# Forgetting attention with the decay tiles in ten buffers, loaded and masked four groups ahead

## Chip, cores and metric

The kernel runs on one core of one Trainium2 chip. The metric is device time in microseconds (us) of one launch. TensorE (PE) multiplies matrices and loads their stationary operand (PEld), VectorE (DVE) and ScalarE (ACT) do the elementwise work, GpSimd (POOL) here issues DMAs and a few additions, SyncE (SP) issues the weight loads.

## What is computed

A two-layer decoder trunk on 256 tokens of width 1024, in float32. Every layer is half a feed-forward block, a token mixer, and another half feed-forward block. The mixer of the second layer, which the change touches, is attention with a learned decay:

```python
decay = transpose(Fqb)[..., None] - F_k[:, :, None, :]      # F: running sums of log forget gates
logits = einsum('bqhd,bkhd->bhqk', qb, k) * scale + decay
logits = where(causal, logits, -inf)
p = softmax(logits, axis=-1)
o = einsum('bhqk,bkhd->bqhd', p, v)                         # then x = x + gate * (o @ w_o)
```

There are 16 heads of width 64, and the queries come in two blocks of 128. The first query block sees 128 keys, the second sees 256, so a head has 384 columns of logits.

## The kernel before

Every large weight matrix streams from HBM in pieces of up to 1024 columns. SP loads a piece into one of six `raw` buffers. ScalarE casts it into a high half `wh` (six buffers), VectorE forms the low half `wl = raw - wh` (five buffers), and each product is three TensorE instructions: high by high, low by high, high by low. TensorE is therefore busy nearly all the time, and the two other engines work as its feeders.

A planner, class `InOrder`, writes out the instructions of TensorE, ScalarE, VectorE and SP in a fixed order. It keeps an estimated clock for each engine and puts casts and `wl` subtractions where it expects an engine to be idle. DMAs issued with `nc.gpsimd` go past it: the compiler's own scheduler places them in POOL's queue, and the planner does not see how long they take.

`attention_b` is the stage of the change. Heads go in pairs; pair `c` is one of eight. First `late_pairs` computes the first half of the queries. Then groups 0 to 9 run. Group `t` is three steps of three pairs at once: the scores of pair `t`, the transposes of the softmax weights of pair `t-1`, and the products with the values of pair `t-2`. Before each group TensorE does `n` steps of fill, `n` being 3, 9, 8, 8, 8, 8, 7, 7, 6, 4 in turn. One step is three matmuls. The first 32 steps compute the rest of the queries (tiles `lq`), and from step 33 on they are the output projection (tiles `pw`, class `OutProj`, which needs the outputs `o[k]`). Four more steps follow group 9, and the last eight are mixed into `OutProj.finish`, which adds the result to `x`.

Within a group the orders are these.

- TensorE: `scores` (tiles `sb`), `values` (into the right half of the bank `wb`), `weights_t`, the six transposes (into `wa` and the left half of `wb`).
- VectorE: four logits passes `d = -0.125 * sb + d` with a row minimum (in `exps`), the low half of the outputs `obl` (in `out_split`), the copy `wtb` (in `weights_out`). Two fill steps before the next group `scale` follows, one reciprocal and four multiplications that finish the softmax in `d`.
- ScalarE: four exponentials (in `exps`), the high half of the outputs `obh` (in `out_split`), the copy `wta` (in `weights_out`).

The decay of head `hd` comes into a tile `d` of 384 columns. Line 1236 loads it from HBM with one POOL DMA (192 KB); line 1241 adds the causal mask to two of its three blocks with a second POOL DMA that accumulates (128 KB, `d<-tri` in the profile). The logits pass then overwrites `d`, the exponentials and `scale` too, and the transposes are its last readers. Six buffers serve the 16 heads, three pairs' worth. They are the hidden tiles of the feed-forward block just before (`hidh4` to `hidh7`, `hidl8`, `hidl9`). `decay(0)` and `decay(1)` stand ahead of group 0 in the code, and group `t` ends with `decay(t + 2)`. Output tiles take `hidh0` to `hidh3` and `hidl4` to `hidl7`.

Of the kernel before, what the change touches and what calls it, by code (L numbers as in the profile page):

```python
# [10 lines left out]
F32 = mybir.dt.float32  # L11
F32R = mybir.dt.float32r
BF16 = mybir.dt.bfloat16
AF = mybir.ActivationFunctionType
ALU = mybir.AluOpType
PSUM = bass.MemoryType.PSUM

P = 128
D = 1024
S = 256  # L20
NC = D // P
# [82 lines left out]
def trunk(ctx, tc, a, out):  # L104
# [4 lines left out]
    dve = InOrder(tc, nc.vector, 0.08, 1 / 960)  # L109
    sp = InOrder(tc, nc.sync, 0.0, 1 / 704)  # L110
    cp_ = ctx.enter_context(tc.tile_pool(name="cp", bufs=1))
# [9 lines left out]
    def sbank(name):  # L121
        return pp.tile([P, 512], F32, tag="s", name=name, bufs=2)

    def abank(name):
        return pp.tile([P, 512], F32, tag="ta", name=name)

    def bbank(name):
        return pp.tile([P, 512], F32, tag="tb", name=name)
# [375 lines left out]
    def late_pair(src, dst, r, name):  # L504

        banks = [mmbank(f"{name}{b}") for b in range(2)]
        blk = take(src)
        for k in range(NC):
            for b in range(2):
                mm3(banks[b][:, :SX], blk(k * 256 + b * P), hx[k], k == 0, k == NC - 1)  # L510
            if k == NC - 1:
                late_out(dst, banks, r)
            yield k, NC

    def late_pairs(src, dsts, m, then):

        pb = []
        for i in range(2):  # L520
            banks = [mmbank(f"lp{i}{b}") for b in range(2)]
            pb.append(banks)
            blk = take(src)
            for k in range(NC):
                for b in range(2):
                    mm3(banks[b][:, :SX], blk(k * 256 + b * P), hx[k], k == 0, k == NC - 1)
                if i == 0:
                    if k == 3:
                        r = rstd_of(then)
                        mh = MakeH(r, m) if m else None  # L530
                else:
                    if k == 0:
                        late_out(dsts[0], pb[0], r)
                    if mh:
                        mh.go()
        if mh:
            mh.go(9 - mh.k)
        late_out(dsts[1], pb[1], r)
        mode[0] = "run"
        return r  # L540
# [366 lines left out]
    for k in range(0, NC, 2):  # L907
# [3 lines left out]
        if k % 4:  # L911
            i = k // 4
# [237 lines left out]
    op, rest = attention_a()  # L1150
# [69 lines left out]
    ffn(1, 0, "ready", None, ((1, 4), (1, 3)))  # L1220

    def attention_b():
        ohs = [cp_.tile([P, 512], F32R, tag=f"hidh{j}", name=f"obh{j}") for j in range(4)]
        ols = [cp_.tile([P, 512], F32R, tag=f"hidl{4 + j}", name=f"obl{j}") for j in range(4)]
        o = [(ohs[c // 2][:, (c % 2) * 256:(c % 2) * 256 + 256],
              ols[c // 2][:, (c % 2) * 256:(c % 2) * 256 + 256]) for c in range(NC)]
        q = [cp_.tile([P, 512], F32, tag=f"hidl{j}", name=f"q{j}") for j in range(4)]
        ds, sms = {}, {}

        DT = [f"hidh{4 + j}" for j in range(4)] + ["hidl8", "hidl9"]  # L1230

        def decay(c):

            for hd in (2 * c, 2 * c + 1):
                d = cp_.tile([P, 384], F32, tag=DT[hd % 6], name=f"d{hd}")
                nc.gpsimd.dma_start(d, bass.AP(fdram.tensor, fdram.offset + hd * (P + S), [[0, P], [1, P + S]]))
                ds[hd] = d
            m2 = mask.rearrange("p (o k) -> p o k", o=1).to_broadcast([P, 2, P])
            for hd in (2 * c, 2 * c + 1):
                diag = ds[hd].rearrange("p (b k) -> p b k", k=P)[:, ::2]  # L1240
                nc.gpsimd.dma_start(diag, m2, accum_op=ALU.add)

        r = late_pairs("wq", q[:2], None, AF.Exp)
        for c in range(2):
            decay(c)
        op = OutProj(o)
        st = {}
        mode[0] = "fill"
        NP = BH // 2

        def scores(c, sb):

            cb = (c % 2) * 256
            for qt, (c0, w) in enumerate(QT):
                for m in range(2):
                    rows = slice(m * HD, m * HD + HD)
                    mm(sb[m][:, c0:c0 + w], q[c // 2][rows, cb + qt * P:cb + qt * P + P],
                       kT[c // 2][rows, cb:cb + w], start=True, stop=True)

        def exps(c, sb):  # L1260
            nm = kp.tile([P, 4], F32, tag="nm", name=f"nmb{c}")
            sm = kp.tile([P, 4], F32, tag="smb", name=f"smb{c}", bufs=3)
            for m in range(2):
                d = ds[2 * c + m]
                for qt, (c0, w) in enumerate(QT):
                    cc = 2 * qt + m
                    dve.tensor_tensor_reduce(
                        d[:, c0:c0 + w], sb[m][:, c0:c0 + w], d[:, c0:c0 + w], -0.125, BIG,
                        ALU.add, ALU.min, accum_out=nm[:, cc:cc + 1])
                    act.activation(d[:, c0:c0 + w], d[:, c0:c0 + w], AF.Exp,  # L1270
                                   bias=nm[:, cc:cc + 1], scale=-1.0, accum_out=sm[:, cc:cc + 1])
            sms[c] = sm

        def scale(c):

            rs = kp.tile([P, 4], F32, tag="rs", name=f"rsb{c}")
            dve.reciprocal(rs, sms[c])
            for m in range(2):
                d = ds[2 * c + m]
                for qt, (c0, w) in enumerate(QT):  # L1280
                    dve.tensor_scalar(d[:, c0:c0 + w], d[:, c0:c0 + w], rs[:, 2 * qt + m:2 * qt + m + 1], None,
                                      op0=ALU.mult)

        def weights_t(c, ta, tb):
            for m, b, to, i in ((0, 0, ta, 0), (0, 1, ta, 1), (0, 2, ta, 2), (1, 2, ta, 3), (1, 0, tb, 0), (1, 1, tb, 1)):
                pe.transpose(to[:, i * P:i * P + P], ds[2 * c + m][:, b * P:b * P + P], ident)

        def weights_out(c, ta, tb):
            w0 = cp_.tile([P, 512], F32, tag="hidh8", name=f"wta{c}")
            w1 = cp_.tile([P, 256], F32, tag="hidh9", name=f"wtb{c}")  # L1290
            act.copy(w0, ta)
            dve.tensor_copy(w1, tb[:, :256])
            st[c] = ((w0[:, :2 * P], w0[:, 2 * P:3 * P]), (w1, w0[:, 3 * P:]))

        def values(c, po):

            for kt in range(2):
                for m in range(2):
                    hd = 2 * c + m
                    v = vb[kt][hd // 8][:, (hd % 8) * HD:(hd % 8) * HD + HD]  # L1300
                    mm(po[m * HD:m * HD + HD, kt * P:], v, st[c][m][kt], start=kt == 0, stop=kt == 1)

        def out_split(c, po):
            oh, ol = o[c]
            act.copy(oh, po)
            dve.tensor_tensor(ol, po, oh.bitcast(F32), op=ALU.subtract)

        def group(t):

            cs, cw, cv = (c if 0 <= c < NP else None for c in (t, t - 1, t - 2))  # L1310
            sb = [sbank(f"sb{t}_{m}") for m in range(2)] if cs is not None else None
            ta = abank(f"wa{t}") if cw is not None else None
            tb = bbank(f"wb{t}") if cw is not None or cv is not None else None
            if cs is not None:
                scores(cs, sb)
            if cv is not None:
                values(cv, tb[:, 256:])
            if cw is not None:
                weights_t(cw, ta, tb)
            if cs is not None:  # L1320
                exps(cs, sb)
            if cv is not None:
                out_split(cv, tb[:, 256:])
            if cw is not None:
                weights_out(cw, ta, tb)
            if t + 2 < NP:
                decay(t + 2)

        def fills():
            for j in (2, 3):  # L1330
                for _ in late_pair("wq", q[j], r, f"lq{j}"):
                    yield
                    yield
            for _ in range(6):
                for _ in op.steps():
                    yield

        fill = fills()
        for t, n in enumerate((3, 9, 8, 8, 8, 8, 7, 7, 6, 4)):
            for i in range(n):  # L1340
                if 1 <= t <= NP and i == n - 2:
                    scale(t - 1)
                next(fill)
            group(t)
        for _ in range(4):
            next(fill)
        return op, fill

    pace[0] = PACE[5]
    op, rest = attention_b()  # L1350
    op.finish((1, 5), ((1, 7), (1, 6)), rest)
    pace[0] = PACE[6]
# [130 lines left out]
```

## Time and profile before

| what | value |
|---|---|
| median of 3 runs | 983.62 us (983.29 to 989.06) |
| the profiled execution's own time | 983.71 us |
| its span in the trace | 981.7 us |
| TensorE busy | 962.2 us, 98% |
| VectorE, ScalarE, POOL busy | 820.0, 552.2, 74.5 us |
| HBM read | 264.75 MB |

The span is the part of the execution that the trace covers; 2.0 us lie around it. "Busy" for TensorE counts overlapping matmuls with modelled ends, so its share says little by itself: the spacing of starts, and the stretches without a start, tell more. In the rows below, a bracket after an instruction gives the idle time of its engine just before it and what ended that time. Windows are given in microseconds from the start of the span.

### The profile page before, as it was taken

Reading aid. Unit: us, or ns where it says so; the run is one execution under the profiler, and the core shown is the slowest. Engines: PE = TensorE matmul, PEld = TensorE weight load, DVE = VectorE, ACT = ScalarE, POOL = GpSimd, SP = SyncE. Lnnn points to the kernel's source line nnn. Section 1 sums busy time; section 2 is a strip of 40 time slices with the busy share of each in tenths; the row PEclk is TensorE's granted clock in tenths of the full one; section 3 lists DMA queues with packets and bytes.
Section 4 is the critical chain, followed back from the end, with each engine's and each line's share of the span. In section 5 each row is a group of like instructions: output and inputs, shape, how many; then the busy total and the mean of one; then the engine's idle time right before and its main releaser. Section 6 shows DMA issues by size and latency. Waiting matters only on the chain.

```text
span 981.7 us, 20425 instructions
## 1 busy us (share of the span) xinstructions
PE 962.2 (98%) x8076; PEld 933.6 (95%) x8076; DVE 820.0 (84%) x1372; ACT 552.2 (56%) x894; POOL 74.5 (8%) x110
## 2 busy tenths in 40 slices
PE   8999999999999999999999999999998799999997
PEld 6999999988999999999998999999997699999997
DVE  7989979889999998878898989889976599555575
ACT  4465545576777654555577545545566476445432
POOL 0000100000112000000000000000044213300000
PEclk9999999999999999999999999999999999999999
DMA  9988999958776699789968999979896437978651
GB/s 361 414 344 279 341 375 343 344 208 289 283 237 229 226 379 371 281 279 319 327 209 318 349 334 326 362 276 338 291 294 155 117 126 214 271 142 278 189 153 43
DMA packets 73825, 270.32 MB, mean 275 GB/s; under 512 B 9673, under 2 KB 14577, under 8 KB 63618
## 3 DMA queue, kind: packets, MB, share of 16 engines
q1 hardware_dynamic: 66016, 259.69, 75.2%
q0 software_dynamic: 7424, 9.02, 4.1%
q8 instruction: 63, 1.03, 0.4%
q10 hardware_dynamic: 290, 0.32, 0.1%
q14 instruction: 32, 0.26, 0.1%
HBM read 264.75 MB, written 2.66 MB: 272 GB/s over the span
## 4 chain that ended last, share of the span: by engine, by line
PE 91%; DVE 3%; issue 3%; DMA 1%; POOL 1%; ACT 1%; DVEq 0%; POOLq 0%; ACTq 0%
PE po L99 25%; PE pg L99 21%; PE pu L99 21%; PE pf L99 5%; PE pv L99 5%; PE lp L99 4%; PE pqk L99 3%; PE pw L99 2%; PE pk L99 1%; DVE wl L99 1%; DMA d<-tri 1%; PE lq L99 1%; DVE HL L99 1%; PE s L99 1%; PE lu L99 1%
## 5 line engine op out<-in xcount | busy, mean ns | idle before, releaser
L99 ACT CAST wh<-raw 128x1024 fp32r<-128x1024 f32 (+1 forms) x360 | 347.3, 975 | 209.9 <-PE pu L99 88.3
L99 DVE TENSOR_TENSOR wl<-raw,wh 128x1024 fp32r<-128x1024 f32 (+1 forms) x360 | 398.5, 1125 | 71.9 <-ACT sg L99 20.7
L99 DVE CUSTOM_DVE_ANT_0 ada<-ada,cact,vecs 128x1024 f32<-128x1024 f32 x160 | 203.4, 1278 | 0.3 <-DMA ada<-in_ada 0.3
L99 PE MATMUL pg<-HH,wl 128*128 128x256 f32 x608 | 168.1, 276 | 0.3 <-DVE wl L99 0.3
L99 PE MATMUL pg<-HH,wh 128*128 128x256 f32 x608 | 168.0, 276 | 0.0
L99 PE MATMUL pu<-HH,wh 128*128 128x256 f32 x608 | 167.9, 276 | 0.0
L99 PE MATMUL pu<-HL,wh 128*128 128x256 f32 x608 | 167.9, 276 | 0.0
L99 PE MATMUL pg<-HL,wh 128*128 128x256 f32 x608 | 167.9, 276 | 0.0
L99 PE MATMUL pu<-HH,wl 128*128 128x256 f32 x608 | 167.9, 276 | 0.0
L99 PE MATMUL po<-hidh,wh 128*128 128x256 f32 x528 | 145.7, 276 | 0.0
L99 PE MATMUL po<-hidh,wl 128*128 128x256 f32 x528 | 145.7, 276 | 0.0
L99 PE MATMUL po<-hidl,wh 128*128 128x256 f32 x528 | 145.7, 276 | 0.0
L99 PEld LDWEIGHTS pg<-HH,wh 128*128 128x128 f32 x608 | 114.1, 188 | 0.7 <-issue 0.6
L99 PEld LDWEIGHTS pg<-HH,wl 128*128 128x128 f32 x608 | 114.2, 188 | 0.5 <-DVE wl L99 0.4
L99 PEld LDWEIGHTS pu<-HH,wh 128*128 128x128 f32 x608 | 114.2, 188 | 0.0
L99 PEld LDWEIGHTS pg<-HL,wh 128*128 128x128 f32 x608 | 114.2, 188 | 0.0
L99 PEld LDWEIGHTS pu<-HL,wh 128*128 128x128 f32 x608 | 114.1, 188 | 0.0
L99 PEld LDWEIGHTS pu<-HH,wl 128*128 128x128 f32 x608 | 114.1, 188 | 0.0
L99 PEld LDWEIGHTS po<-hidh,wh 128*128 128x128 f32 x528 | 99.1, 188 | 0.0
L99 PEld LDWEIGHTS po<-hidh,wl 128*128 128x128 f32 x528 | 99.1, 188 | 0.0
L99 PEld LDWEIGHTS po<-hidl,wh 128*128 128x128 f32 x528 | 99.1, 188 | 0.0
L99 ACT CAST hidh<-hf 128x512 fp32r<-128x512 f32 x44 | 27.3, 621 | 40.8 <-DVE hf L99 40.6
(224 smaller groups left out, 1864.7 us busy)
## 6 DMA issues: line engine op xcount, KB each, us to landing
raw<-in_win SPq DMA_DIRECT2D x176, 512.0 KB, 6.7
ada<-in_ada SPq DMA_DIRECT2D x79, 1024.0 KB, 6.9
raw<-in_wout SPq DMA_DIRECT2D x48, 384.0 KB, 5.6
raw<-in_wout SPq DMA_DIRECT2D x48, 320.0 KB, 5.1
raw<-in_wqk SPq DMA_DIRECT2D x16, 512.0 KB, 5.3
raw<-in_wo SPq DMA_DIRECT2D x16, 512.0 KB, 5.8
raw<-in_wlast SPq DMA_DIRECT2D x16, 512.0 KB, 4.1
raw<-in_wv SPq DMA_DIRECT2D x8, 512.0 KB, 7.3
```

Source lines behind the costliest of these rows:

```text
L99: return self.tc.keep_in_program_order(f(*args, **kw))
```

## The change

- The decay tiles get ten buffers in place of six. The four new ones are `hidh2`, `hidh3`, `hidl6` and `hidl7`, which the last two output tiles take later; output tiles are now allocated when they are first written (`o_tiles`).
- Load and mask are separate functions. Ahead of group 0 the loads of pairs 0 to 4 and their masks are issued, loads one pair ahead of masks. Groups 1, 2 and 3 end with load and mask of pairs 5, 6 and 7.
- The copy `obh` on ScalarE moves ahead of the exponentials of the group, and the subtraction `obl` on VectorE moves behind the copy `wtb`.

```diff
-        ohs = [... tag=f"hidh{j}" ... for j in range(4)]
-        ols = [... tag=f"hidl{4 + j}" ... for j in range(4)]
+        o = {}
+
+        def o_tiles(j):
+            h = cp_.tile([P, 512], F32R, tag=f"hidh{j}", name=f"obh{j}")
+            l = cp_.tile([P, 512], F32R, tag=f"hidl{4 + j}", name=f"obl{j}")
+            for i in range(2):
+                o[2 * j + i] = h[:, i * 256:i * 256 + 256], l[:, i * 256:i * 256 + 256]
...
-        DT = [f"hidh{4 + j}" for j in range(4)] + ["hidl8", "hidl9"]
+        DT = ["hidh4", "hidh5", "hidh6", "hidh7", "hidl8", "hidl9", "hidh2", "hidh3", "hidl6", "hidl7"]
...
-                d = cp_.tile([P, 384], F32, tag=DT[hd % 6], name=f"d{hd}")
+                d = cp_.tile([P, 384], F32, tag=DT[hd % 10], name=f"d{hd}")
...
+        def masked(c):
+
             m2 = mask.rearrange("p (o k) -> p o k", o=1).to_broadcast([P, 2, P])
...
-        for c in range(2):
+        decay(0)
+        for c in range(1, 5):
             decay(c)
+            masked(c - 1)
+        masked(4)
...
         def out_split(c, po):
+            if c % 2 == 0:
+                o_tiles(c // 2)
             oh, ol = o[c]
             act.copy(oh, po)
-            dve.tensor_tensor(ol, po, oh.bitcast(F32), op=ALU.subtract)
+            return lambda: dve.tensor_tensor(ol, po, oh.bitcast(F32), op=ALU.subtract)
...
+            low = out_split(cv, tb[:, 256:]) if cv is not None else None
             if cs is not None:
                 exps(cs, sb)
-            if cv is not None:
-                out_split(cv, tb[:, 256:])
             if cw is not None:
                 weights_out(cw, ta, tb)
-            if t + 2 < NP:
-                decay(t + 2)
+            if low:
+                low()
+            if cw is not None and t + 4 < NP:
+                decay(t + 4)
+                masked(t + 4)
```

More of the change, by code (lines that the diff above doesn't have):

```diff
@@ L1222, in attention_b @@
     def attention_b():
[L1223 to L1226, printed above, removed]
+        o = {}
[4 more added lines that the diff above has]
+                o[2 * j + i] = h[:, i * 256:i * 256 + 256], l[:, i * 256:i * 256 + 256]
         q = [cp_.tile([P, 512], F32, tag=f"hidl{j}", name=f"q{j}") for j in range(4)]
         ds, sms = {}, {}
-        DT = [f"hidh{4 + j}" for j in range(4)] + ["hidl8", "hidl9"]
+        DT = ["hidh4", "hidh5", "hidh6", "hidh7", "hidl8", "hidl9", "hidh2", "hidh3", "hidl6", "hidl7"]
         def decay(c):
             for hd in (2 * c, 2 * c + 1):
-                d = cp_.tile([P, 384], F32, tag=DT[hd % 6], name=f"d{hd}")
+                d = cp_.tile([P, 384], F32, tag=DT[hd % 10], name=f"d{hd}")
                 nc.gpsimd.dma_start(d, bass.AP(fdram.tensor, fdram.offset + hd * (P + S), [[0, P], [1, P + S]]))
                 ds[hd] = d
+        def masked(c):
             m2 = mask.rearrange("p (o k) -> p o k", o=1).to_broadcast([P, 2, P])
```

## The prediction

> **What bounds the kernel now.** I first read the timeline of TensorE, to find where each group's scores start, and then asked for one window from each start to the next. Columns: length, busy time and count of PE, PEld, DVE, ACT and POOL, granted clock, DMA share, GB/s.
>
> ```profile
> 742.81:750.19 7.38, 5.57 (x47) 4.59 (x46) 5.12 (x21) 4.16 (x16) 2.79 (x5) 1.00 0.83 216
> 750.19:755.39 5.20, 5.20 (x47) 4.42 (x46) 2.49 (x12) 2.84 (x10) 2.28 (x5) 1.00 0.66 120
> 755.39:761.78 6.39, 5.38 (x45) 4.18 (x44) 4.08 (x14) 2.75 (x8) 2.86 (x4) 1.00 0.87 189
> 761.78:769.42 7.64, 5.72 (x45) 4.46 (x44) 4.26 (x16) 3.66 (x11) 3.60 (x4) 1.00 0.71 178
> 769.42:778.58 9.16, 5.14 (x42) 4.15 (x41) 5.70 (x24) 5.39 (x17) 2.46 (x2) 1.00 0.34 66
> 778.58:793.65 15.07, 15.07 (x119) 14.12 (x120) 10.80 (x21) 9.48 (x19) 2.96 (x4) 0.89 0.34 105
> ```
>
> These are groups 3 to 7, then groups 8 and 9 with the rest of the stage. Equal work takes 5.20 us once and 9.16 us at the end. What it costs when TensorE never waits comes from stretches that ran freely:
>
> ```profile
> 713.78 0.28 PE L99 MATMUL po<-hidh,wl 128*128 128x256 f32 x1
> ...
> 715.25 0.28 PE L99 MATMUL po<-hidl,wh 128*128 128x256 f32 x1
> ...
> 727.39 0.29 PE L99 MATMUL lq<-HH,wh 128*128 128x258 f32 x1
> ...
> 728.72 0.28 PE L99 MATMUL lq<-HL,wh 128*128 128x258 f32 x1
> ...
> 737.45 0.93 PE L99 MATMUL sb<-kT,q 64*128 64x128 f32 x8
> 738.30 0.43 PE L99 MATMUL wb<-wta,vb 128*64 128x256 f32 x1
> ...
> 739.10 0.66 PE L99 MATMUL wa<-tri,d 128*128 128x128 f32 x4
> ...
> 739.73 0.37 PE L99 MATMUL lq<-HH,wh 128*128 128x258 f32 x1
> ```
>
> From the first `po` to the last are 13 starts, 0.113 us each, so a projection step of three matmuls takes 0.34 us. The `lq` rows span 11 starts, 0.121 us each, so a query step takes 0.36 us. A group takes 2.28 us: scores 0.85, values 0.80, transposes 0.63. The free periods are then 2.28 + 4 x 0.36 + 4 x 0.34 = 5.1 for group 3, 2.28 + 8 x 0.34 = 5.0 for group 4, 2.28 + 7 x 0.34 = 4.7 for groups 5 and 6, and 2.28 + 6 x 0.34 = 4.3 for group 7. From group 8 on there remain 0.80 + 0.63, four steps, 0.80, twelve steps and 48 matmuls of `finish`: 1.43 + 1.36 + 0.80 + 4.08 + 5.44 = 13.1. Against the windows TensorE loses 2.3, 0.2, 1.7, 3.0, 4.8 and 2.0 us, **14.0 us in all**. That is the most the stage can give.
>
> What ends the waits I took from VectorE's timeline:
>
> ```profile
> 761.68 0.29 DVE L99 CUSTOM_DVE_ANT_0 d<-sb,d 128x128 f32<-128x128 f32 x1 [2.28 <-DMA d<-tri]
> ...
> 769.97 0.29 DVE L99 CUSTOM_DVE_ANT_0 d<-sb,d 128x128 f32<-128x128 f32 x1 [2.92 <-DMA d<-tri]
> ...
> 775.98 0.29 DVE L99 CUSTOM_DVE_ANT_0 d<-sb,d 128x128 f32<-128x128 f32 x1 [1.32 <-DMA d<-tri]
> ```
>
> The logits passes of groups 5, 6 and 7 stand still for the mask. The reader is to see a queue that runs late, here POOL's:
>
> ```profile
> 711.63 1.90 POOL L1236 DMA_DIRECT2D d<-fdram  x3 [185.25 <-PE po L99]
> ...
> 716.08 1.27 POOL L1241 DMA_DIRECT2D d<-tri  x1 [1.66 <-DMA d<-fdram]
> 718.27 1.21 POOL L1241 DMA_DIRECT2D d<-tri  x1 [0.92 <-DMA d<-fdram]
> 719.02 1.06 POOL L1236 DMA_DIRECT2D d<-fdram  x1
> 720.51 2.42 POOL L1241 DMA_DIRECT2D d<-tri  x2 [0.44 <-DMA d<-fdram]
> ...
> 726.31 1.17 POOL L1241 DMA_DIRECT2D d<-tri  x1 [2.79 <-DMA d<-fdram]
> 732.42 1.19 POOL L1241 DMA_DIRECT2D d<-tri  x1 [4.94 <-DMA d<-fdram]
> ...
> 741.35 2.14 POOL L1236 DMA_DIRECT2D d<-fdram  x2
> ...
> 770.78 2.46 POOL L1241 DMA_DIRECT2D d<-tri  x2 [3.90 <-DMA d<-fdram]
> ```
>
> From the load pair at 741.35 to the end of the last mask pair, 773.24, are four rounds: 8.0 us a round, in which POOL mostly waits for a load to land before it can issue the mask. A free group needs 4.3 to 5.1 us. With six buffers a round cannot start before the transposes of three pairs back, so nothing is ever ahead.
>
> **The ten buffers.** The same 16 loads and 16 masks are issued; ten of each now stand ahead of group 0. Two rows show that POOL's queue is ordered by readiness and not by the text: three loads come before the first mask, and the load at 719.02 belongs to a call behind group 0, whose scores start at 728.93. So I expect the early loads to run ahead, as their buffers are old hidden tiles. Ten loads cost 0.63 us (1.90 / 3) to 1.06 us each and ten masks 1.23 us (half of 2.46): 18.6 to 22.9 us. With the first landing waits, 1.66 + 0.92, the early part ends between 732.8 and 737.1. Pairs 5 to 7 take a serial round of 8.0 us each and end at 761.1 at the latest; the last logits pass began 2.7 us after the last mask issue had ended (773.24 to 775.98), so all masks are there by 763.8. Group 7 will want its second tile at about 766.7 (below). The mask waits go, with 2.9 us to spare. DMA bandwidth does not forbid it: the share in the windows above is 0.34 to 0.87, and only what is early is crowded.
>
> **The copy `obh` ahead of the exponentials.** It is the same instruction, but it adds a wait: behind it in ScalarE's queue stand the exponentials and `wta`. How long it waits is seen where it waited before:
>
> ```profile
> 780.80 0.63 PE L99 MATMUL wb<-tri,d 128*128 128x128 f32 x2
> ...
> 781.47 0.37 ACT L99 CAST obh<-wb 128x256 fp32r<-128x256 f32 x1 [3.42 <-PE wb L99]
> ```
>
> It starts when the last transpose into `wb` is done, not after the values, so 2.3 us after the start S of a group. Below are exponentials, softmax scaling and a `wl`:
>
> ```profile
> 737.47 1.01 DVE L99 TENSOR_SCALAR d<-d,rsb 128x128 f32<-128x128 f32 x4
> ...
> 739.52 1.22 DVE L99 TENSOR_TENSOR wl<-raw,wh 128x1024 fp32r<-128x1024 f32 x1
> ...
> 738.74 0.40 ACT L99 ACTIVATE d<-d,nmb 128x128 f32<-128x128 f32 x1 [0.78 <-DVE nmb L99]
> ...
> 740.51 0.35 ACT L99 CAST obh<-wb 128x256 fp32r<-128x256 f32 x1
> ```
>
> Exponentials take 1.8 us (738.74 to 740.51). Before, they began at S + 1.3; now at S + 2.7, ending at S + 4.5. Scaling ends near S + 5.6. TensorE wants these tiles at S + 4.7 + 0.85 + 0.80 = S + 6.3 with seven steps of fill: hidden, with 0.7 us to spare. If the cover is gone (a second `wl` of 1.2 us before the scaling), it costs 0.5 us a group. `wta` ends at S + 5.1 and is wanted at S + 5.5. In group 8 there are no scores ahead of the values, so they are wanted at 2.28 + 2.04 = S + 4.3: I charge **0.8 us** there. For near misses I charge **0.2 us** in each of groups 4 to 7, 0.8 us; the bounds are 0 and 0.5 each.
>
> **The subtraction `obl` last.** VectorE loses its wait for `obh`. That is cover, not path, except through `scale`, already counted.
>
> **The stall in group 3.** It is not one for decays:
>
> ```profile
> 749.30 0.39 PE L99 MATMUL pw<-obh,wh 128*128 128x256 f32 x1 [1.81 <-DVE lt L99]
> ```
>
> The projection waits for a bank that `lt` frees, which stands behind exponentials, `obh` and `wta` on ScalarE. The new order moves that queue no earlier, as the exponentials now wait for `obh`. I take no gain, nearest to the row; the bounds are 0 and 2.3.
>
> **The clock.** Two windows around the start of group 8:
>
> ```profile
> 774.00:778.60 4.60, 2.23 (x22) 2.06 (x20) 3.23 (x13) 2.72 (x10) 0.00 (x0) 1.00 0.21 25
> 778.80:782.20 3.40, 3.40 (x19) 2.92 (x16) 1.08 (x5) 0.73 (x2) 0.00 (x0) 0.50 0.46 153
> ```
>
> Half the clock for 3.4 us is 1.7 of the 2.0 us lost from group 8 on; it followed a stretch in which TensorE was idle half the time. With that stretch gone it should not come.
>
> The Trainium skill ("TensorE: Matmul & The Clock Gate", What's actually happening) lets the clock fall only after a whole idle window of about 3.4 us. Here 22 matmuls started in the 4.6 us before, so the trace does not agree; by the rule alone a short mask wait would never cost clock, by the trace it may add 1.7 us.
>
> **The sum.** Of the 14.0 us I leave 2.3 (group 3), 0.2 (group 4), 0.8 (group 8), 0.8 (near misses) and 0.5 for a first mask that is late in one group, 4.6 in all: a gain of 9.4 us. The profiled execution took 983.71 us, 0.09 above the median of 983.62, so **974.3 us**. By these terms the groups start at 750.2, 755.4, 760.3 and 765.1, hence the 766.7 above (group 7's second tile is read 1.6 us after its start). One per cent, 9.8 us, is about what a measurement of this kernel can tell from no change; the forecast sits just inside it.
>
> **Rivals.**
>
> *TensorE hardly waits at all.* If group 3's bank also comes free in time and group 8 does not wait, 2.3 + 0.5 more: about 971.5, at the limit 969.7. For it: group 3's logits passes began at 745.45 just as its masks landed. Against it: ScalarE's longer chain.
>
> *The POOL queue stays the bound, only shorter.* The early loads meet the stream of weights. If all five landing waits quoted come again (1.66 + 0.92 + 0.44 + 2.79 + 4.94 = 10.75), the early part ends at 711.63 + 20.7 + 10.75 = 743.1, pair 7 lands at 769.8, and group 7 is 3.1 us late: 977.4, or 979.1 with the clock.
>
> ```profile
> L1236 POOL DMA_DIRECT2D d<-fdram x16: 538/1054/1572, 711.6 to 765.8; - x16
> L1241 POOL DMA_DIRECT2D d<-tri x16: 1172/1228/1723, 716.1 to 771.5; - x16
> ```
>
> With each of the twenty issues at its longest, 32.9 us, the early part ends at 747.1, group 7 is 7.1 us late: 981.4.
>
> The Trainium skill ("SBUF — State Buffer", Who interferes with whom) names a cause: VectorE's copies and `tensor_scalar` may lock GpSimd out while it writes descriptors. These rows, with a longest issue 0.5 us above the median, bear it out little.
>
> *The gain is given back in `finish`,* if VectorE comes there with a backlog: 980 to 983. Against it, VectorE itself waited for TensorE there:
>
> ```profile
> 785.55 1.23 DVE L99 TENSOR_TENSOR wl<-raw,wh 128x1024 fp32r<-128x1024 f32 x1 [0.54 <-PE pw L99]
> ```
>
> *Slower: a new loop.* Transposes, `obh`, exponentials, scaling and the next transposes now form a ring: 0.3 + 1.8 + 1.0 + 0.6 and releases, about 4.1 us. A `wh` cast ahead of `obh` or a late `wl` adds 1.0 to 1.2 us each. It decides above 7.2 us, the mean of the five windows from 742.81 to 778.58; with four such additions it is 8.5 us, 6.7 us more in five groups: 990. Against it, a feeding piece is needed only once in eight steps.
>
> **How the numbers follow.** Forecast 0.46 (own range 972 to 977), free TensorE 0.17, POOL late 0.23, given back 0.07, slower 0.07. Faster by over 1% (under 973.9) are the free case and 0.45 of the forecast, 0.38; slower by over 1% is 0.06; the rest 0.56. The range from 969.5 to 982.0 leaves out the slower case and the ends of two others.
>
> **What would show it.** Right: no logits pass waits for `d<-tri` in groups 5 to 7, periods near 5 us there, clock 1.00 after group 8, `obh` waiting for `wb` in every group. Wrong: POOL's last mask issued after 764, or scaled tiles late for the transposes in most groups.

## The result, and the profile after

| | before | after |
|---|---|---|
| median (5 runs each) | 984.19 us (983.29 to 989.83) | 974.78 us (973.48 to 976.91) |
| profiled execution, its span | 983.71, 981.7 us | 973.79, 972.0 us |
| the stage, from the first `lp` of the attention to the first `lg` behind it | 78.25 us | 67.67 us |

The ratio is 0.9888, with an interval of 0.9852 to 0.9924: 9.4 us faster. The forecast was 974.3 us.

First, the same windows of the changed kernel as were shown of before: groups 3 to 7, then groups 8 and 9 with the rest of the stage. Columns as there.

```profile
743.74:750.36 6.62, 5.56 (x47) 4.58 (x47) 4.96 (x17) 4.38 (x16) 3.30 (x4) 1.00 0.73 178
750.36:755.56 5.20, 5.20 (x47) 4.43 (x47) 3.91 (x19) 3.58 (x13) 2.20 (x3) 1.00 0.83 199
755.56:760.42 4.86, 4.86 (x44) 4.09 (x44) 4.71 (x16) 3.21 (x11) 1.89 (x4) 1.00 0.95 172
760.42:765.28 4.86, 4.86 (x44) 4.09 (x44) 3.50 (x17) 3.55 (x12) 2.37 (x2) 1.00 0.94 220
765.28:770.51 5.23, 4.59 (x42) 3.75 (x41) 4.43 (x19) 3.86 (x12) 0.00 (x0) 1.00 0.37 98
770.51:783.93 13.42, 13.42 (x118) 12.65 (x119) 10.48 (x21) 9.42 (x19) 2.95 (x4) 1.00 0.27 86
```

The periods fall from 7.38, 5.20, 6.39, 7.64, 9.16 and 15.07 us; the gains are 0.76, 0, 1.53, 2.78, 3.93 and 1.65 us. The clock of the last row is 1.00 where it was 0.89. Where PE's busy time equals the window, the trace shows no stand-still of TensorE: that holds for groups 4, 5 and 6 and from group 8 on.

POOL's queue in the timeline of after:

```profile
711.21 1.90 POOL L1240 DMA_DIRECT2D d<-fdram  x3 [183.88 <-PE po L99]
...
717.50 1.28 POOL L1248 DMA_DIRECT2D d<-tri  x1 [3.54 <-DVE x L99]
...
726.05 2.47 POOL L1248 DMA_DIRECT2D d<-tri  x2 [2.45 <-DMA d<-fdram]
...
730.75 2.39 POOL L1248 DMA_DIRECT2D d<-tri  x2 [1.64 <-DMA d<-fdram]
...
739.56 1.18 POOL L1248 DMA_DIRECT2D d<-tri  x1 [3.00 <-DVE d L99]
740.26 1.67 POOL L1240 DMA_DIRECT2D d<-fdram  x2
747.06 2.48 POOL L1248 DMA_DIRECT2D d<-tri  x2 [5.13 <-DMA d<-fdram]
...
760.32 2.47 POOL L1248 DMA_DIRECT2D d<-tri  x2 [2.97 <-DMA d<-fdram]
```

The queue still waits for landings; only now it does so ahead of time. The early part, ten loads and ten masks, ends at 740.74 (739.56 + 1.18), and three serial rounds run from 740.26 to 762.79. The issue of the last mask pair ends 10.45 us earlier than before (762.79 against 773.24).

Selected rows of the timeline of after on the other engines: what TensorE waits for, the high half of the outputs, the scaling of group 5 and, in group 7, the first logits pass on each of its two decay tiles, which waited 0.56 and 1.32 us for their masks in the kernel before:

```profile
749.48 0.38 PE L99 MATMUL pw<-obh,wh 128*128 128x256 f32 x1 [1.06 <-DVE lt L99]
...
770.51 0.43 PE L99 MATMUL wb<-wta,vb 128*64 128x256 f32 x1 [0.64 <-ACT wta L99]
...
758.13 0.37 ACT L99 CAST obh<-wb 128x256 fp32r<-128x256 f32 x1 [1.65 <-PE wb L99]
...
760.77 1.20 DVE L99 TENSOR_SCALAR d<-d,rsb 128x128 f32<-128x128 f32 x4
...
766.29 0.29 DVE L99 CUSTOM_DVE_ANT_0 d<-sb,d 128x128 f32<-128x128 f32 x1
...
767.98 0.29 DVE L99 CUSTOM_DVE_ANT_0 d<-sb,d 128x128 f32<-128x128 f32 x1
```

From group 3 to the start of group 8 TensorE's matmuls have only these two waits, 1.06 and 0.64 us. These two passes of group 7 have no bracket: their decay is there. No wait for `d<-tri` is left on VectorE in the whole stage.

### The profile page after: what moved, and what is told of

It reads as the page before. It is cut to its first block, busy times and chain, and to the rows that moved or that the text cites. A ratio compares the mean times of both kernels' runs of the same rounds, so it can differ in the third digit from the quotient of the medians.

```text
span 972.0 us, 20418 instructions
## 1 busy us (share of the span) xinstructions
PE 959.7 (99%) x8076; PEld 933.5 (96%) x8076; DVE 819.8 (84%) x1372; ACT 551.8 (57%) x894; POOL 74.6 (8%) x110
## 3 DMA queue, kind: packets, MB, share of 16 engines
q8 instruction: 63, 1.03, 0.4%
## 4 chain that ended last, share of the span: by engine, by line
PE 94%; DVE 3%; issue 1%; ACT 1%; POOL 0%; ACTq 0%; DVEq 0%; POOLq 0%
PE po L99 25%; PE pg L99 21%; PE pu L99 21%; PE pf L99 5%; PE pv L99 5%; PE lp L99 4%; PE pqk L99 3%; PE pw L99 3%; PE pk L99 1%; PE lq L99 1%; DVE wl L99 1%; PE wb L99 1%; DVE HL L99 1%; PE s L99 1%; PE sb L99 1%
```

## The experiments

Three theories were put against each other. **A:** the ten buffers give the gain, because masks land before they are needed; the new order of `obh` and `obl` gives nothing. **B:** the new order gives a good part of it. **C:** it is not the number of buffers but the early place of the calls. "The stage" is measured as in the table above.

### Buffers without the new order

The high and low halves go back behind the exponentials and ahead of `weights_out`; all else is as after.

```diff
-            return lambda: dve.tensor_tensor(ol, po, oh.bitcast(F32), op=ALU.subtract)
+            dve.tensor_tensor(ol, po, oh.bitcast(F32), op=ALU.subtract)
...
-            low = out_split(cv, tb[:, 256:]) if cv is not None else None
             if cs is not None:
                 exps(cs, sb)
+            if cv is not None:
+                out_split(cv, tb[:, 256:])
             if cw is not None:
                 weights_out(cw, ta, tb)
-            if low:
-                low()
```

> Only the ten buffers and the early loads and masks; outputs are written in the old order (exponentials, obh, then obl, wtb). Theory A, the gain is the end of the mask waits: 973.5 to 977, no logits pass waits for d<-tri in groups 5 to 7. Theory B, the gain comes from the new order of the output copies (VectorE waited 6.2 us for obh before): 982 to 985.

Measured: 973.42 us, ratio 0.9897 (0.9877 to 0.9916). The row of the whole stage and those of groups 3 to 6:

```profile
715.45:782.50 67.05, 66.18 (x564) 59.31 (x563) 52.22 (x160) 47.97 (x128) 29.54 (x32) 1.00 0.78 207
...
742.89:749.43 6.54, 5.77 (x47) 4.59 (x46) 5.18 (x22) 4.06 (x16) 3.62 (x4) 1.00 0.93 233
749.43:754.63 5.20, 5.20 (x47) 4.43 (x46) 4.60 (x15) 4.58 (x12) 2.76 (x4) 1.00 0.42 99
754.63:759.49 4.86, 4.86 (x44) 4.09 (x43) 3.54 (x17) 3.35 (x11) 0.89 (x2) 1.00 1.05 258
759.49:764.35 4.86, 4.86 (x44) 4.09 (x43) 3.53 (x16) 3.00 (x12) 2.36 (x2) 1.00 0.71 197
```

The buffers alone give the whole gain: 11.2 us of the stage (78.25 - 67.05), and the same periods of 5.20 and 4.86 us. The waits of VectorE in this kernel show that the cover of the new order is not needed, and how near POOL is to its limit:

```profile
DVE obl L99 <- ACT obh L99: 5.3, 5, 1.3
...
DVE d L99 <- DMA d<-tri: 0.3, 1, 0.3
```

VectorE still waits 5.3 us for `obh`, and it costs nothing: the only wait of TensorE's matmuls from group 3 on is one of 0.77 us, for `lt`. The 0.3 us is the first pass on group 7's second tile. Rows of the timeline: TensorE's wait, POOL's last issue and that pass.

```profile
748.53 0.38 PE L99 MATMUL pw<-obh,wh 128*128 128x256 f32 x1 [0.77 <-DVE lt L99]
...
761.99 2.47 POOL L1248 DMA_DIRECT2D d<-tri  x2 [6.47 <-DMA d<-fdram]
...
766.45 0.29 DVE L99 CUSTOM_DVE_ANT_0 d<-sb,d 128x128 f32<-128x128 f32 x1 [0.30 <-DMA d<-tri]
```

### The new order without the buffers

On before's code, so with its six buffers and its calls of `decay`:

```diff
-            dve.tensor_tensor(ol, po, oh.bitcast(F32), op=ALU.subtract)
+            return lambda: dve.tensor_tensor(ol, po, oh.bitcast(F32), op=ALU.subtract)
...
+            low = out_split(cv, tb[:, 256:]) if cv is not None else None
             if cs is not None:
                 exps(cs, sb)
-            if cv is not None:
-                out_split(cv, tb[:, 256:])
             if cw is not None:
                 weights_out(cw, ta, tb)
+            if low:
+                low()
```

> Only the new order of the output copies, with six buffers and decay two groups ahead as before. Theory A: no gain, 982 to 988, logits passes of groups 5 to 7 still wait 2 to 3 us for d<-tri, and the half clock comes again before group 8. Theory B: 974 to 978.

Measured: 980.9 us, ratio 0.9967 (0.9948 to 0.9986): below the range expected by A and above the one expected by B. The stage takes 75.32 us, 2.9 less than before. In its timeline the mask is still late, here in groups 6 and 7:

```profile
767.46 0.29 DVE L99 CUSTOM_DVE_ANT_0 d<-sb,d 128x128 f32<-128x128 f32 x1 [3.77 <-DMA d<-tri]
...
769.09 0.29 DVE L99 CUSTOM_DVE_ANT_0 d<-sb,d 128x128 f32<-128x128 f32 x1 [0.99 <-DMA d<-tri]
```

The views of waits, before's line first, show TensorE's weight load of the values waiting less for `wta`:

```profile
PEld wb L99 <- ACT wta L99: 5.9, 4, 2.5
```

```profile
PEld wb L99 <- ACT wta L99: 2.0, 2, 1.4
```

So B holds only where the masks are late: there the order saves 2.9 us. That the shorter wait for `wta` is the cause is argued, not shown: the last mask pair also ends 1.1 us earlier (772.17 against 773.24). The clock takes part of the gain back. It falls twice in this stage, from 750.0 and from 770.5 us, where in before it falls once. The second fall:

```profile
770.50:773.90 3.40, 3.24 (x16) 2.26 (x16) 2.35 (x8) 1.32 (x2) 1.67 (x2) 0.50 0.64 80
```

With ten buffers the order saves nothing; the stage is 0.6 us longer with it (67.67 against 67.05), the size of the 0.64 us wait in group 8. The two gains do not add up.

### Ten buffers, calls placed as before

```diff
-        decay(0)
-        for c in range(1, 5):
+        for c in range(2):
             decay(c)
-            masked(c - 1)
-        masked(4)
+            masked(c)
...
-            if cw is not None and t + 4 < NP:
-                decay(t + 4)
-                masked(t + 4)
+            if t + 2 < NP:
+                decay(t + 2)
+                masked(t + 2)
```

> The changed kernel with ten buffers, but the calls of load and mask stand where they stood before (pairs 0 and 1 ahead of group 0, pair t + 2 at the end of group t). Theory A, POOL's queue is ordered by when a buffer is free and not by the place of the call: within 1.5 us of the changed kernel, 973.5 to 976.5. Theory C, it is the calls four groups ahead that count: a round of 8 us and 2.7 us of landing in two periods of 4.9 us are late, 978 to 984.

Measured: 974.47 us, ratio 0.9905 (0.9886 to 0.9924), stage 67.67 us, equal to after. C falls: the place of the calls in the code does not matter. POOL's queue shows why:

```profile
731.09 1.64 POOL L1240 DMA_DIRECT2D d<-fdram  x2
...
759.40 2.48 POOL L1248 DMA_DIRECT2D d<-tri  x2 [2.76 <-DMA d<-fdram]
```

By the count of loads ahead of it, the first row holds those of pair 4. Their calls stand at the end of group 2, whose scores start at 738.58, yet they go out 7.5 us ahead of that. So the place of a call does not hold a load back; a free buffer lets it go early.

### Six buffers, no masks

This asks what POOL's queue still costs with ten buffers. The kernel leaves the causal mask out, so it computes another attention, and only its time is of use.

```diff
-            m2 = mask.rearrange("p (o k) -> p o k", o=1).to_broadcast([P, 2, P])
-            for hd in (2 * c, 2 * c + 1):
-                diag = ds[hd].rearrange("p (b k) -> p b k", k=P)[:, ::2]
-                nc.gpsimd.dma_start(diag, m2, accum_op=ALU.add)
```

(on before's code)

> The kernel before with the causal mask left out (loads alone, six buffers, decay two groups ahead, old order of the copies). Theory A: the masks were what the stage waited for, so this comes to 973 to 977, and how far it lies below the changed kernel is what POOL's queue still costs there (I expect under 1.5 us). Theory B: 982 to 985.

Measured: 972.65 us, ratio 0.9893 (0.9869 to 0.9916), stage 66.96 us. That is 0.1 us less than with ten buffers and all masks in the old order (67.05). The masks' whole cost on the path, 11.3 us before (78.25 - 66.96), is gone with ten buffers.

### Eight buffers

On the first experiment's code: `hidh10` and `hidl10` in place of the four new tiles, four pairs ahead of group 0, the rest three groups ahead.

```diff
-        DT = [..., "hidl8", "hidl9", "hidh2", "hidh3", "hidl6", "hidl7"]
+        DT = [..., "hidl8", "hidl9", "hidh10", "hidl10"]
...
-                d = cp_.tile([P, 384], F32, tag=DT[hd % 10], name=f"d{hd}")
+                d = cp_.tile([P, 384], F32, tag=DT[hd % 8], name=f"d{hd}")
...
-        for c in range(1, 5):
+        for c in range(1, 4):
...
-        masked(4)
+        masked(3)
...
-            if cw is not None and t + 4 < NP:
-                decay(t + 4)
-                masked(t + 4)
+            if cw is not None and t + 3 < NP:
+                decay(t + 3)
+                masked(t + 3)
```

> Ten buffers become eight (hidh10 and hidl10 in place of hidh2, hidh3, hidl6, hidl7), pairs 0 to 3 early, pair t + 3 at the end of group t, outputs in the old order as in the buffers-only kernel (stage of 67.0 us, 973.4). Theory A, POOL goes through a pair in a serial round of 7.5 to 8.0 us against 4.9 of a group, and buffers only decide how many pairs are ahead at the start: four serial rounds from about 736 end at 766 to 768, landing 2.7 later, 2.7 to 4.7 late for group 7: 976 to 978.5, with a wait for d<-tri in group 7 and little before. Theory D, any cover over three pairs is enough, since a round is shorter than two groups: 973 to 974.5, no such wait.

Measured: 981.88 us, ratio 0.9969 (0.9945 to 0.9993), stage 72.97 us. Rows of its timeline, VectorE then TensorE:

```profile
769.19 0.29 DVE L99 CUSTOM_DVE_ANT_0 d<-sb,d 128x128 f32<-128x128 f32 x1 [3.87 <-DMA d<-tri]
...
773.04 0.40 PE L99 MATMUL wb<-wta,vb 128*64 128x256 f32 x1 [4.37 <-DVE rsb L99]
```

And its windows around the wait:

```profile
770.40:773.80 3.40, 0.76 (x8) 0.57 (x8) 3.32 (x12) 1.83 (x8) 0.00 (x0) 0.99 0.13 20
773.80:777.20 3.40, 3.40 (x19) 3.34 (x17) 1.57 (x4) 1.76 (x3) 0.00 (x0) 0.50 0.36 136
```

The mask is late in group 7 alone, by 3.87 and 0.61 us. TensorE stands, and then runs 3.4 us at half clock, in which 1.7 us of work are lost. The stage is 5.9 us longer than with ten (72.97 - 67.05): 4.5 us are the waits, and the 1.4 us left are near the clock's 1.7. The place was as expected; the time, 976 to 978.5, was not. The clock had been left out of it, and the last feed-forward of this profiled execution ran slower too (512 matmuls from 850 to 910 us, a window that is shown below under the projection steps). Whether its other runs were slow for the same reason is not known. Two buffers less than ten thus cost half of the stage's gain (5.9 of 11.2 us).

### Every mask twice

On the first experiment's code: each of the 16 mask DMAs is issued a second time.

```diff
-                nc.gpsimd.dma_start(diag, m2, accum_op=ALU.add)
+                for _ in range(2):
+                    nc.gpsimd.dma_start(diag, m2, accum_op=ALU.add)
```

> The buffers-only kernel with every mask added twice (twice -1e30 masks as once does). It takes the cover away: a second issue of 1.23 us for each tile and a wait for the first mask to land, so POOL's round of 7.5 to 8 us becomes 13 to 15. Theory A: pairs 5 to 7 and the early masks are late together, 985 to 1005, with long waits for d<-tri. If POOL has far more room than I think: under 978.

Measured: 993.93 us, ratio 1.0113 (1.0077 to 1.0149): 1.1% slower than before. Its waits and two windows:

```profile
DVE d L99 <- DMA d<-tri: 11.5, 4, 3.8
```

```profile
737.60:744.50 6.90, 6.27 (x29) 5.86 (x29) 2.95 (x15) 3.01 (x10) 6.90 (x7) 0.51 1.09 207
...
782.00:785.40 3.40, 3.40 (x20) 2.94 (x17) 0.99 (x6) 0.18 (x1) 2.17 (x2) 0.50 0.71 89
```

With POOL's queue made longer, ten buffers no longer cover it, and the clock falls as well. A is borne out from the other side.

### Group 3: another order of the first projection steps

On the first experiment's code. Step `n` writes the bank `n % 4`, and the first step of bank 2, which in the first experiment waits for `lt`, now comes fifth in place of third, behind the scores of group 4. (Bank 3 is met by the seventh step as before, and not one step later as the expectation has it.)

```diff
-            for n in range(NC) if k else (0, 1, 2, 4, 5, 6, 3, 7):
+            for n in range(NC) if k else (0, 1, 4, 5, 2, 6, 3, 7):
```

> The buffers-only kernel with another order of the first eight projection steps (0, 1, 4, 5, 2, 6, 3, 7 in place of 0, 1, 2, 4, 5, 6, 3, 7), so that the two banks which wait for lt are touched two steps, 0.68 us, and one step later. If the wait in group 3 is that for the bank: the stage from the first lp to the first lg falls from 67.0 to 66.2 to 66.4, time 972.3 to 973.2. If another wait is just behind it: stage 66.8 to 67.1.

Measured: 975.27 us, ratio 0.9913 (0.988 to 0.9947), stage 66.42 us. Group 3 takes 5.33 us (scores start at 743.18 and 748.51) in place of 6.54, and TensorE no longer waits for `lt`, so the bank was the cause of its stall. But group 6 now takes 5.35 us (758.57 to 763.92) in place of 4.86: there the scaling comes late, behind a wait for `obh` and a `wl`. The stage is 0.6 us shorter, and the total shows no gain. The same code run once more:

> The bank-order kernel once more, unchanged. Its profile had 427 matmuls in the 50 us from 850, where the others but one had 443, at a granted clock of 1.00, and lost 3.9 us in the last feed-forward block by that. If the pace belongs to the kernel's code: again 427 and a span of 974. If it differs from one execution to the next: 443 about as often, a span of 970 and times that fall into two groups 3 to 4 us apart.

It took 976.92 us, ratio 0.991 (0.9883 to 0.9936), stage 66.84 us. The shorter stage comes back, the shorter time does not. In this execution 3.0 us were lost before 200 us of the span, where nothing was changed (the first `lp` matmul of the whole kernel starts at 200.6, against 197.6 in the first of the two). One window in the last feed-forward, first of the first of these runs, then of the second:

```profile
850.00:910.00 60.00, 60.00 (x512) 60.00 (x511) 32.06 (x33) 29.42 (x34) 0.00 (x0) 1.00 0.77 199
```

```profile
850.00:910.00 60.00, 60.00 (x531) 60.00 (x530) 33.80 (x34) 31.09 (x35) 0.00 (x0) 1.00 0.78 208
```

At a granted clock of 1.00 in both, the same instructions go 3.6% slower in the first (512 against 531). The two ran on different chips, but the chip does not decide it: on the chip of the first, the kernel with eight buffers has 512 in this window and the one with every mask twice 531; and from 50 to 100 us it is the second that is slow, with 427 matmuls against 440, again at a clock of 1.00. What sets this pace stays open. In the 60 us shown it is worth 2.1 us (60 x 19 / 531), more than the 0.6 us in question.

### Both repairs together

On after: the exponentials go ahead of `obh` again, `obl` stays last, and the bank order is as above.

```diff
-            low = out_split(cv, tb[:, 256:]) if cv is not None else None
             if cs is not None:
                 exps(cs, sb)
+            low = out_split(cv, tb[:, 256:]) if cv is not None else None
...
-            for n in range(NC) if k else (0, 1, 2, 4, 5, 6, 3, 7):
+            for n in range(NC) if k else (0, 1, 4, 5, 2, 6, 3, 7):
```

> Ten buffers, exponentials ahead of obh on ScalarE as before, obl behind wtb on VectorE, and the bank order of the experiment before. It takes out VectorE's wait for obh (up to 1.3 us a group), which made the softmax scaling late in group 6 there. If that wait was the cause: stage from the first lp to the first lg 65.7 to 66.1 (66.4 before, 67.0 with buffers only), group 6 back to 4.9, and a time of 971 to 973. If not: 66.3 to 66.6.

Measured: 974.54 us, ratio 0.9897 (0.987 to 0.9924), stage 68.55 us. The expectation failed. Its waits:

```profile
DVE wtb L99 <- ACT obh L99: 7.3, 6, 1.3
...
PEld wa L99 <- DVE d L99: 3.7, 10, 1.0
```

The wait for `obh` did not go with `obl`: the copy `wtb`, which reads the same bank `wb`, waits for it in its place, and then `scale` and the transposes are late (3.7 us). So leaving `obl` last is no repair, and whether the wait for `obh` was what made group 6 late stays open. None of these kernels beats after by more than the runs can tell; the first experiment has the lowest median of those with all masks.

## Why the prediction was right, point by point

**The sum.** It foresaw a gain of 9.4 us. The medians give 9.41 (984.19 - 974.78), the profiled executions 9.92 (983.71 - 973.79). The agreement is partly luck: the stage gave 10.6 us (78.25 - 67.67), and the profiled execution of after was 1.0 us behind already at 198 us of the span, where nothing was changed (the first `lp` starts at 198.7, before at 197.7). There TensorE's clock had stood at 0.50 from 14.7 to 18.1 us, in before at 1.00; but the first experiment has such a stretch too and starts its first `lp` at 197.8, so where the 1.0 us came from is not shown.

**Ten buffers: right in cause, mis-sized in the queue.** The early part was to end between 732.8 and 737.1; it ended at 740.74. The term that was too small is the landing waits: two were counted, 1.66 + 0.92, but 2.45 and 1.64 us came behind them, and the 3.00 us ahead of the mask at 739.56. The loads did not all run ahead. The rounds were a little shorter, 7.5 us ((762.79 - 740.26) / 3) in place of 8.0, and the last issue ended 1.7 us later than the latest time given. The spare was to be 2.9 us. In the first experiment the pass that did wait began 2.0 us after the last issue had ended (766.45 - 764.46), where 2.7 were reckoned; by that, after's masks were all there at 764.8. The second tile of group 7 was read at 767.98, so the spare was 3.2 us. That it did not shrink is partly luck: VectorE did a `wl` of 1.22 us between the two tiles, and without it the pass would have come near 766.8, with 2.0 us to spare. In the first experiment, where the pass came earlier, there was no spare at all. The rival "POOL late" was near: with ten buffers and each mask added once, the waits that the traces put down to `d<-tri` stay at or under 0.4 us, but with eight buffers it happened, and it cost more than its 3.1 us.

**`obh` ahead of the exponentials: right.** It waits for `wb` in all eight groups that have it, and starts at S + 2.6 in group 5 (758.13 - 755.56), where 2.3 was reckoned. The scaling there ends at S + 6.4, two `wl` having come before it, and the transposes begin at S + 6.5 (weights of `wa` at 762.08). The spare is 0.1 us, not 0.7, and no transpose's weights waited more than 0.3 for `d`. The wait of group 8's values, at the end of the fifth window, is 0.64 us where 0.8 was charged. The slower rival, the ring, did not decide, and nothing was given back in `finish`: TensorE never stands still in the last window.

**Near misses: right size, wrong name.** Groups 4, 5 and 6 take 0.2 us more than the free periods that the prediction reckoned (5.20 for 5.0, 4.86 for 4.7). But TensorE is busy throughout in them, and the first experiment, with the old order, has the same 5.20 and 4.86. The 0.2 us belong to the group itself; the free period had been reckoned too short.

**The stall in group 3: mis-sized.** 2.3 us were kept; 1.5 remained (6.62 - 5.1). The step that failed is "no gain": it looked at ScalarE's order alone. The wait for `lt` fell from 1.81 to 1.06 us in after and to 0.77 us with the buffers alone, so it is masks that come in time, not the order, that move `lt` forward. This is part of the rival "hardly waits at all", which the row at 745.45 had spoken for.

**The clock: right.** No half clock in the stage after. The last window is within 0.3 us of the free 13.1, so the 1.7 us are gone.

**The mask that is late in one group: not needed.** The 0.5 us left for it was not lost.

**The new order as a whole.** That it brings nothing was right with ten buffers. With six it shortened the stage by 2.9 us, which the prediction did not see, as it never asked what each part does alone.

## What to carry to other kernels

Where an engine waits for a chain of two dependent DMAs, measure the round of the chain and compare it with the period of the loop: more buffers do not make the round shorter, they let it start earlier, and the lead to reckon with is (round - period) times the rounds that must still be made. A wait that stands behind the real bound, such as `obl` for `obh` here, can be taken away without any gain, and its fix can cost when the bound is gone; try each part alone. Count a short stall of TensorE together with the clock that it may cost.

## What the runs showed of the hardware that was not expected

**Half clock without an idle window.** Windows of before: first one with a long stall that was followed by no fall of the clock, then the 3.4 us ahead of the stretch at half clock, and that stretch. Then the stretch and the window ahead of it in the kernel with the new order alone:

```profile
748.10:751.50 3.40, 2.20 (x18) 1.63 (x20) 2.83 (x12) 2.47 (x7) 3.40 (x4) 1.00 0.53 87
...
775.40:778.80 3.40, 1.03 (x10) 0.84 (x10) 2.78 (x10) 1.73 (x6) 0.00 (x0) 1.00 0.01 4
778.80:782.20 3.40, 3.40 (x19) 2.92 (x16) 1.08 (x5) 0.73 (x2) 0.00 (x0) 0.50 0.46 153
```

```profile
746.60:750.00 3.40, 1.38 (x12) 1.18 (x11) 2.56 (x12) 2.56 (x11) 3.40 (x4) 1.00 0.60 143
750.00:753.40 3.40, 3.40 (x21) 2.15 (x19) 3.06 (x13) 1.35 (x3) 0.27 (x2) 0.51 1.09 218
```

Half clock followed 3.4 us in which TensorE was busy for 0.76 (eight buffers), 1.03 and 1.38 us; it did not follow 2.20 us. A single stall of 2.0 us was enough in the second kernel (3.40 - 1.38). Busy time alone does not draw the line: with every mask twice, half clock followed a window of 1.79 us (768.37 to 771.77), and with eight buffers it did not follow one of 1.72 (766.95 to 770.35, just ahead of the one that it did follow). The Trainium skill ("TensorE: Matmul & The Clock Gate", What's actually happening) lets the clock fall after an idle window of about 3.4 us; the stretches at half clock here last about as long, but that the window ahead must be idle throughout these rows do not bear out.

**A pace that differs by 3.6% at the same granted clock** between two executions of the same code, as shown above.

**A copy on VectorE that waits for ScalarE's read of the same bank** (`wtb` for `obh`, 7.3 us in six waits); whether the chip needs that order, or only the program asks for it, no run here shows.
